# Addresses, one number of a build-time list and the pace of the modulation steps, in a two-layer decoder trunk on one core

## The chip, the cores and the metric

One NeuronCore of a Trainium2 chip runs the whole program. Its engines work side by side: TensorE (PE in the profile, with its weight loads as PEld), VectorE (DVE), ScalarE (ACT), GpSimd (POOL), and SyncE (SP), which issues the transfers from HBM. The metric is device microseconds of one execution.

## The reference

Two layers, 256 tokens, 1024 channels, everything in float32. In short:

```python
for l in range(DEPTH):                                   # DEPTH = 2
    mod = c_act @ w_ada[l] + b_ada[l]                    # 1024 x 6144, one row
    sh1, sc1, g1, sh2, sc2, g2 = split(mod, 6)
    h = rms_norm(x, norm1_g[l]) * (1 + sc1) + sh1
    q, k, v, iq, ik, iw, z, xbc, dt_raw, ga, gm = split(h @ w_in[l])      # 10856 columns
    o_attn = dsa_attention(...) @ w_attn_o[l]            # 64 keys kept of each query's causal ones
    o_ssm  = rms_norm((ssd_scan(...) + xs * d_skip) * silu(z)) @ w_ssm_o[l]
    x = x + g1 * ((sigmoid(ga) * o_attn + sigmoid(gm) * o_ssm) @ w_out[l])
    h = rms_norm(x, norm2_g[l]) * (1 + sc2) + sh2
    val, gate = split(causal_dwconv(h @ w_up[l]))        # 2 x 2816 columns
    x = x + g2 * ((silu(gate) * val) @ w_down[l])
```

## The kernel before, in words

**Products.** Every large weight matrix streams through once. A unit is a piece of 512 rows by 512 columns (four blocks of 128 rows); SP loads it into `st`. ScalarE rounds it to float32r (`wh`, line 783) and VectorE takes the rest (`wl = st - wh`, line 784). Both rings have three buffers:

```python
hi = wpool.tile([P, u["nk"], u["n"]], F32R, tag="wh", name=f"wh{cnt[0]}", bufs=3)
lo = wpool.tile([P, u["nk"], u["n"]], F32R, tag="wl", name=f"wl{cnt[0]}", bufs=3)
```

Activations are split in the same way, and each product of two float32 values is three matmuls: high by high, low by high, high by low. In `run_fm` the weights are the stationary operand and 256 tokens move (twelve matmuls for one block of 128 output columns in one unit); in `run_tm` the activations are stationary and 512 weight columns move. The program has 8112 such matmuls; below they are called products. Their order is fixed by the plan of the layers, so the number of products issued is a clock of the program that both versions share.

**The order of everything else** is made at build time. Each operation on ScalarE, VectorE and GpSimd becomes a `Work` with an estimated duration (`takes`), and `plan_ahead` lays these out in time on each engine against TensorE's own time `now`, which `on_pe` advances by a price for each matmul (`after`, line 392). For a float32r product of 256 columns this price was 9.5 + 0.4258 x 256 = 118.5 ns. `commit` then issues the work in the order of its planned starts. No duration of this list reaches the chip: it only decides the order in which instructions stand in each engine's queue, and each engine works through its own queue strictly in order.

**Side tasks** (turns of q and k by transposes, attention, the state-space part, norms) are generators. `pump`, called after every twelve products or so, resumes one when the list believes its operands ready (`Need.due`).

**Modulation.** Four of the twelve 512-column pieces of layer 0's `w_ada` are done at the start; the other 20 pieces (8 of layer 0, 12 of layer 1) run as a stream in the background, `ada_stream` at line 1011. A piece is eight steps: a 256 KB load `ad` and one VectorE operation `adacc = ad * c + adacc`. Then TensorE sums over the partitions (the fold, `bk<-adacc,ones`), ScalarE copies the row out (`adarow<-bk`), and TensorE turns it (`bk<-ident,adarow`). How many steps should be done by which pump is the table `GOALS` (line 714).

**Places in SBUF.** Tiles get fixed byte addresses by the order and the size of their allocation. In the built program, `wh` and `wl` start at 32 modulo 256 in every partition; the activations `h` (first norm's output and others) and `u` at 224, which is 192 further on; `xdt` (it also holds the last two operands of two products in each layer), `cbm` and `text` at 160; `ones` at 128.

Of the kernel before, what the change touches and what calls it, by code (L numbers as in the profile page):

```python
# [10 lines left out]
F32 = mybir.dt.float32  # L11
# [11 lines left out]
KT = 8  # L23
# [23 lines left out]
def trunk(ctx, tc, x, c, positions, w_ada, b_ada, norm1_g, w_in, q_norm_g, k_norm_g, ssm_conv_w, ssm_conv_b,  # L47
# [22 lines left out]
    class Work:  # L70


        __slots__ = ("key", "ns", "pr", "deps", "least", "start", "end", "done", "issue", "share", "soft")

        def __init__(self, key, ns, deps, least, issue):
            number[0] += 1
            self.key, self.ns, self.pr, self.deps, self.least = key, ns, number[0] - boost[0], deps, least
            self.start, self.end, self.done, self.issue = None, None, False, issue
            self.share, self.soft = 1.0, 0.0

    def region(x):

# [101 lines left out]
    def commit(edge=None):  # L184

        plan_ahead()
        edge = now[0] - LEAD_IN if edge is None else edge
        for key, ws in waiting.items():
            for w in sorted(ws, key=lambda w: w.start):
                if w.start < edge:  # L190
                    w.done = True
                    w.deps = ()
                    free_at[key] = max(w.start + 0.4 * w.ns, w.end - LAP[key])
                    if w.share < 1.0:
                        at_port[key == "pool"] = w
                    begun.append(w)
            ws[:] = [w for w in ws if not w.done]
        begun.sort(key=lambda w: (w.start, w.pr))
        n = 0
        while n < len(begun) and begun[n].start < edge:  # L200
            begun[n].issue()  # L201
            begun[n].issue = None
            n += 1
        del begun[:n]

    def end_of(w, by=None):
        if not w.done:
# [184 lines left out]
    def after(prev, cur):  # L392

        kind, n, shape = prev
        ns = 92.0 if shape != cur[2] else 0.0
        if kind == "r":
            return ns + 9.5 + 0.4258 * max(n, S)
        if kind in "bt":
            return ns + (2.5 + 0.832 * n if kind == "t" else 173.0)
        if shape == (128, 128):  # L400
            return ns + (143.0 if n <= 32 else 16.0 + 1.617 * n)
        if shape == (128, 32):
            return ns + 21.0
        return ns + (0.85 * n if shape == (128, 64) else 0.95 * n if n == S else 163.0)

    slow_until = [0.0]

    def on_pe(o, lhsT, rhs, issue, turn=False):
        n, rows, cols = rhs.free_size(), lhsT.partition_size(), lhsT.free_size()
# [80 lines left out]


    ident = cst.tile([P, P], F32, name="ident")
    ones = cst.tile([P, P], F32, name="ones")
    V.memset(ones, 1.0)
    G.affine_select(ident, ones, pattern=[[-1, P]], compare_op=ALU.is_equal, fill=0.0, base=0, channel_multiplier=1)
    mhalf = cst.tile([P, 2], F32, name="mhalf")
    G.memset(mhalf, -0.5)


# [33 lines left out]
    SP.dma_start(crow, c.rearrange("b (r q) -> (b r) q", q=P))  # L533
    pc = bank()
    T.transpose(pc[:, 0:KT], crow, ident[0:KT, 0:KT])
    csil = cst.tile([P, KT], F32, name="csil")
    gate_act = A.activation(csil, pc[:, 0:KT], AF.Tanh, scale=0.5)
    V.scalar_tensor_tensor(csil, csil, 1.0, pc[:, 0:KT], op0=ALU.add, op1=ALU.mult)
    chalf = cst.tile([P, KT], F32, name="chalf")
    V.tensor_scalar(chalf, csil, 0.5, None, op0=ALU.mult)  # L540
    crep = hold(w_tile("cv", [P, S])).rearrange("p (k n) -> p k n", n=32)
    crep_ins = V.tensor_scalar(crep, csil[:, :, None].to_broadcast([P, KT, 32]), 0.5, None, op0=ALU.mult)
# [4 lines left out]
    class Link:  # L547
# [73 lines left out]
        def finish(self, ev):  # L621

            def features(m, ps):
                settle(lambda: self.r is not None)
                bias = w_tile("bcol", [P, 1])
                if self.i == 0:
                    y = ev(m, None)
                    with urgent(FIRST):
                        V.tensor_scalar(bias, ps[:, S:S + 1], 0.5, None, op0=ALU.mult)
                        V.tensor_tensor(y, ps[:, 0:S], self.r, op=ALU.mult)  # L630
                        A.activation(y, y, AF.Tanh, scale=0.5, bias=bias)
                else:
# [78 lines left out]
    MARGIN = 11000.0  # L711


    GOALS = ((44, 0), (224, 50), (364, 98), (618, 147), (720, 161))
    LEAD = 6
    ADA_LATE = -30
    ADA_GAP = 7000.0
# [610 lines left out]
    def mixer(l, link, link_out):  # L1328
# [40 lines left out]
        def use_misc(ps):  # L1369
# [24 lines left out]
            def dt_task():  # L1394
# [29 lines left out]
                mm(pa[:, 0:32], uext[:, 0:P], adt[:, 0, 0:32], True, False)  # L1424
                mm(pa[:, 32:64], ones, adt[:, 0, 0:32], False, False)
                mm(pa[:, 32:64], uext[:, 0:P], adt[:, 1, 0:32], False, True)
                acs = w_tile("acs", [P, 2, 32], F32, 1)
                A.activation(acs.rearrange("p t h -> p (t h)"), pa[:, 0:64], AF.Copy)
                pb = bank()
                mm(pb[0:64, 0:S], adt[:, 0, :], uext, True, False)  # L1430
# [498 lines left out]
```

## Time and profile before

| | us |
|---|---|
| median of three runs (1241.02 to 1243.19) | 1241.21 |
| the profiled execution | 1240.05 |
| its span, from the first to the last instruction | 1238.3 |

| engine | busy us | share of the span | instructions |
|---|---|---|---|
| PE | 1206.7 | 97% | 9833 |
| PEld | 1122.9 | 91% | 9833 |
| DVE | 991.0 | 80% | 1549 |
| ACT | 776.7 | 63% | 1397 |
| POOL | 475.5 | 38% | 503 |

The profile lists rows of one engine as start, duration, engine, line, operation, what is written and what is read (`out<-in`), how many equal ones follow each other, and in brackets the engine's idle time before, with what ended it. Nearly all rows stand at L201, the line at which `commit` issues, so they are told apart by tile names. Matmuls overlap: what one costs is the distance from its start to the next start, not its duration. In layer 0 the first mixer runs from about 20 to 445 us and the FFN to 645 us; layer 1 follows, with its FFN from about 1045 us.

### The profile page before, as it was taken

The numbers are of one execution on the slowest core, as the hardware profiler recorded it, in microseconds if no ns is written. First come the engines' busy times: TensorE is split into PE (matmuls) and PEld (weight loads), VectorE is DVE, ScalarE is ACT, GpSimd is POOL, SyncE is SP. The second block draws the span as 40 slices with busy tenths as digits, with TensorE's granted clock in tenths as the row PEclk, the third lists the DMA queues.
The fourth block names the chain that finished last, engine by engine and source line by source line (L and its number), as shares of the span: only waits on it lengthen the run. The fifth ranks groups of instructions, "written<-read, shape, count | busy, mean of one in ns | idle before, by whom it ended". The sixth has DMA issues, their size and how long they took to land.

```text
span 1238.3 us, 24795 instructions
## 1 busy us (share of the span) xinstructions
PE 1206.7 (97%) x9833; PEld 1122.9 (91%) x9833; DVE 991.0 (80%) x1549; ACT 776.7 (63%) x1397; POOL 475.5 (38%) x503
## 2 busy tenths in 40 slices
PE   8999999999999999999999999999999999999898
PEld 7777888999999999999997777899999999999898
DVE  5599998877977789989777998888788677887762
ACT  4465667775774478776364566877588435877732
POOL 2162623342343226675121554405416222556510
PEclk9999999999999999999999999999999999999999
DMA  9854644556565748777847555444665665556551
GB/s 301 277 201 145 220 161 146 177 194 210 191 221 198 257 143 260 246 230 244 284 145 258 176 191 193 150 163 164 207 214 168 217 226 179 166 185 211 198 188 58
DMA packets 158665, 246.55 MB, mean 199 GB/s; under 512 B 11868, under 2 KB 66870, under 8 KB 158549
## 3 DMA queue, kind: packets, MB, share of 16 engines
q1 hardware_dynamic: 157989, 244.77, 59.6%
q8 instruction: 77, 1.26, 0.4%
q14 instruction: 39, 0.32, 0.1%
q0 software_dynamic: 288, 0.19, 0.1%
q10 hardware_dynamic: 272, 0.00, 0.0%
HBM read 243.89 MB, written 1.05 MB: 198 GB/s over the span
## 4 chain that ended last, share of the span: by engine, by line
PE 77%; DVE 12%; ACT 5%; POOL 3%; issue 3%; DMA 0%; DVEq 0%; ACTq 0%; POOLq 0%
PE bk L201 77%; DVE wl L201 5%; DVE w L201 3%; POOL w L201 2%; ACT wh L201 2%; ACT w L201 2%; DVE adacc L201 1%; DVE t L201 1%; DVE u L201 1%; POOL rr L201 0%; DVE mx L201 0%; ACT u L201 0%; DVE p L201 0%; POOL rows L201 0%; DVE sp_p L201 0%
## 5 line engine op out<-in xcount | busy, mean ns | idle before, releaser
L201 PE MATMUL bk<-h,wh 128*128 128x256 f32 x3296 | 591.5, 282 | 1.2 <-ACT h L201 1.1
L201 PEld LDWEIGHTS bk<-h,wh 128*128 128x128 f32 x3296 | 502.1, 189 | 11.4 <-issue 8.6
L201 DVE TENSOR_TENSOR wl<-st,wh 128x2048 fp32r<-128x2048 f32 (+1 forms) x200 | 440.5, 2209 | 84.5 <-ACT wh L201 84.1
L201 PE MATMUL bk<-h,wl 128*128 128x256 f32 x1648 | 459.5, 279 | 1.2 <-DVE wl L201 1.2
L201 ACT ACTIVATE wh<-st 128x2048 fp32r<-128x2048 f32 (+1 forms) x200 | 352.9, 1770 | 151.3 <-PE bk L201 117.6
L201 POOL TENSOR_TENSOR w<-w,w 128x254 f32<-128x254 f32 (+2 forms) x213 | 253.8, 1205 | 322.4 <-DVE w L201 223.7
L201 PEld LDWEIGHTS bk<-h,wl 128*128 128x128 f32 x1648 | 310.8, 189 | 2.8 <-DVE wl L201 2.4
L201 PE MATMUL bk<-u,wh 128*128 128x256 f32 x1312 | 233.4, 281 | 0.0
L201 PEld LDWEIGHTS bk<-u,wh 128*128 128x128 f32 x1312 | 199.4, 189 | 2.2 <-issue 2.2
L201 PE MATMUL bk<-u,wl 128*128 128x256 f32 x656 | 182.9, 279 | 0.0
L201 ACT ACTIVATE w<-bk,vec 128x256 f32<-128x256 f32 (+2 forms) x256 | 118.4, 519 | 55.7 <-DVE w L201 37.0
L201 PE MATMUL bk<-wh,h 128*128 128x512 f32 x448 | 146.6, 404 | 3.1 <-ACT wh L201 2.0
L201 PEld LDWEIGHTS bk<-u,wl 128*128 128x128 f32 x656 | 123.6, 188 | 0.0
L201 DVE SCALAR_TENSOR_TENSOR adacc<-ad,chalf,adacc 128x512 f32<-128x512 f32 x140 | 120.3, 860 | 2.7 <-DMA ad<-in_w_ada_dram 1.2
L201 PEld LDWEIGHTS bk<-wh,h 128*128 128x128 f32 x448 | 82.5, 189 | 24.1 <-issue 3.5
L201 DVE SCALAR_TENSOR_TENSOR w<-bk,vec,w 128x255 f32<-128x255 f32 (+1 forms) x176 | 79.9, 475 | 21.5 <-ACT w L201 19.6
L201 PE MATMUL bk<-wl,h 128*128 128x512 f32 x224 | 89.0, 397 | 3.0 <-DVE wl L201 3.0
L201 POOL TENSOR_TENSOR u<-u,u 128x256 f32<-128x256 f32 (+1 forms) x56 | 61.7, 1120 | 58.3 <-DVE u L201 30.4
L201 POOL TENSOR_TENSOR rr<-ss,mhalf 128x16 f32<-128x16 f32 x8 | 33.6, 4195 | 75.8 <-DVE ss L201 75.7
L201 ACT ACTIVATE u<-bk 128x128 f32<-128x128 f32 (+2 forms) x128 | 32.4, 327 | 36.3 <-PE bk L201 36.3
L201 PEld LDWEIGHTS bk<-wl,h 128*128 128x128 f32 x224 | 42.5, 190 | 13.3 <-DVE wl L201 4.5
L201 POOL TENSOR_SCALAR p<-p,sums 128x128 f32<-128x128 f32 x64 | 36.6, 590 | 33.9 <-DVE sums L201 33.9
(225 smaller groups left out, 1386.5 us busy)
## 6 DMA issues: line engine op xcount, KB each, us to landing
st<-in_w_in_dram SPq DMA_DIRECT2D x80, 1024.0 KB, 5.2
st<-in_w_up_dram SPq DMA_DIRECT2D x88, 512.0 KB, 4.7
ad<-in_w_ada_dram SPq DMA_DIRECT2D x160, 256.0 KB, 5.3
st<-in_w_down_dram SPq DMA_DIRECT2D x20, 1024.0 KB, 6.5
st<-in_w_ssm_o_dram SPq DMA_DIRECT2D x16, 1024.0 KB, 5.3
st<-in_w_ada_dram SPq DMA_DIRECT2D x16, 512.0 KB, 9.3
st<-in_w_attn_o_dram SPq DMA_DIRECT2D x8, 1024.0 KB, 5.1
st<-in_w_out_dram SPq DMA_DIRECT2D x8, 1024.0 KB, 5.2
```

The costliest lines, as they stand in the source:

```text
L201: begun[n].issue()
```

## The change

The diff has four parts.

- **Addresses.** Three small constants are allocated earlier, `bcol` gets eight buffers, `acs` is 80 instead of 64 wide, and a spacer of 256 bytes stands ahead of the `u` tiles. In the built program this moves `xdt`, `cbm` and `text` from 160 to 224 and `ones` from 128 to 224 modulo 256; `wh`, `wl`, `h` and `u` keep theirs.
- **The list's price of a product** falls from 118.5 to 114.0 ns (5.0 instead of 9.5).
- **`GOALS`**: 66 instead of 50 modulation steps by pump 224, and 98 by pump 350 instead of 364.
- **`commit`** issues an operation only after those it needs; before, equal or later planned starts of a needed one could stand behind.

```diff
-        begun.sort(key=lambda w: (w.start, w.pr))
-        n = 0
-        while n < len(begun) and begun[n].start < edge:
-            begun[n].issue()
...
+        for w in begun:
+            w.turn = w.start, w.pr
+        begun.sort(key=lambda w: w.turn)
+        while begun and begun[0].turn[0] < edge:
+            w = begun.pop(0)
+            late = [(d.turn or (d.start, d.pr))[0] for d in w.needs if d.issue]
+            if late:
+                w.turn = max(max(late), w.turn[0]) + 0.5, w.pr
+                insort(begun, w, key=lambda w: w.turn)
+                continue
+            w.issue()
...
-            return ns + 9.5 + 0.4258 * max(n, S)
+            return ns + 5.0 + 0.4258 * max(n, S)
...
+    mhalf = cst.tile([P, 2], F32, name="mhalf")
+    csil = cst.tile([P, KT], F32, name="csil")
+    chalf = cst.tile([P, KT], F32, name="chalf")
     ones = cst.tile([P, P], F32, name="ones")
...
-                bias = w_tile("bcol", [P, 1])
+                bias = w_tile("bcol", [P, 1], bufs=8)
...
-    GOALS = ((44, 0), (224, 50), (364, 98), (618, 147), (720, 161))
+    GOALS = ((44, 0), (224, 66), (350, 98), (618, 147), (720, 161))
...
+        pools["u"].tile([P, 64], F32, tag="front", name="front_u", bufs=1)
...
-                acs = w_tile("acs", [P, 2, 32], F32, 1)
+                acs = w_tile("acs", [P, 80], F32, 1)[:, 0:64].rearrange("p (t h) -> p t h", t=2)
```

All work stays the same; where it stands changes on every engine. Three places are shown. In the kernel before issued instructions stand at L201, in the changed one at L209; the numbers in the names differ between the versions.

The first is ScalarE's queue at the border of the layers, at the first full unit behind the 128-column pieces of layer 1 (the row with 128x2048). `wh` rows are splits, `u<-bk` rows copy q's turned index heads out of PSUM. Before:

```order
L201 ACTIVATE wh_8450<-st_8173 128x512
L201 ACTIVATE u_8481<-bk_8502 128x128
L201 ACTIVATE u_8482<-bk_8502 128x128
L201 ACTIVATE u_8483<-bk_8502 128x128
L201 ACTIVATE u_8484<-bk_8502 128x128
L201 ACTIVATE wh_8491<-st_8286 128x2048
```

Now, with the same split as `wh_8522`:

```order
L209 ACTIVATE wh_8476<-st_8192 128x512
L209 ACTIVATE wh_8522<-st_8306 128x2048
L209 ACTIVATE u_8512<-bk_8533 128x128
L209 ACTIVATE u_8513<-bk_8533 128x128
L209 ACTIVATE u_8514<-bk_8533 128x128
L209 ACTIVATE u_8515<-bk_8533 128x128
```

The split went ahead of the four copies. TensorE's queue at the same border, where `ident,t` rows are the transposes of a turned part of q. Before:

```order
L201 MATMUL bk_8489<-h_8285,wh_8450 128x256
L201 MATMUL bk_8489<-h_8284,wl_8451 128x256
L201 MATMUL bk_8522<-ident,t_1193_8487 128x128 x4
L201 MATMUL bk_8524<-wh_8491,h_8250 128x512
L201 MATMUL bk_8524<-wh_8491,h_8251 128x512
L201 MATMUL bk_8524<-wl_8492,h_8250 128x512
```

Now:

```order
L209 MATMUL bk_8520<-h_8305,wh_8476 128x256
L209 MATMUL bk_8520<-h_8304,wl_8477 128x256
L209 MATMUL bk_8552<-wh_8522,h_8269 128x512
L209 MATMUL bk_8552<-wh_8522,h_8270 128x512
L209 MATMUL bk_8552<-wl_8523,h_8269 128x512
L209 MATMUL bk_8552<-wh_8522,h_8272 128x512
L209 MATMUL bk_8552<-wh_8522,h_8273 128x512
L209 MATMUL bk_8552<-wl_8523,h_8272 128x512
L209 MATMUL bk_8592<-ident,t_1197_8518 128x128 x4
```

Four transposes that stood ahead of the full unit's first products stand behind six of them.

The second is ScalarE's queue at the last modulation row, in layer 1's FFN: `w<-bk` rows are the two taps of the FFN's convolution for four blocks of a chunk (`bk_14623` and `bk_14624` before hold two blocks each). Before:

```order
L201 ACTIVATE u_14604<-w_2105_14603 128x256
L201 ACTIVATE w_2114_14716<-bk_14623,vec_1593 128x256
L201 ACTIVATE w_2115_14717<-bk_14623,vec_1593 128x254
L201 ACTIVATE w_2116_14718<-bk_14623,vec_1593 128x256
L201 ACTIVATE w_2117_14719<-bk_14623,vec_1593 128x254
L201 ACTIVATE w_2118_14748<-bk_14624,vec_1593 128x256
L201 ACTIVATE w_2119_14749<-bk_14624,vec_1593 128x254
L201 ACTIVATE w_2123_14753<-bk_14624,vec_1593 128x256
L201 ACTIVATE w_2124_14754<-bk_14624,vec_1593 128x254
L201 ACTIVATE adarow_14775<-bk_14774 128x128
```

Now:

```order
L209 ACTIVATE w_2105_14604<-w_2103_14602 128x256
L209 ACTIVATE w_2114_14713<-bk_14621,vec_1560 128x256
L209 ACTIVATE w_2115_14714<-bk_14621,vec_1560 128x254
L209 ACTIVATE w_2116_14715<-bk_14621,vec_1560 128x256
L209 ACTIVATE w_2117_14716<-bk_14621,vec_1560 128x254
L209 ACTIVATE w_2118_14746<-bk_14622,vec_1560 128x256
L209 ACTIVATE w_2119_14747<-bk_14622,vec_1560 128x254
L209 ACTIVATE adarow_14770<-bk_14769 128x128
L209 ACTIVATE u_14605<-w_2105_14604 128x256
```

The row's copy stands behind six taps instead of eight, and the split of the activation `u` that stood ahead of them stands behind it.

The third is VectorE's queue in the first mixer, near product 1700 of 8112 (around 340 us before): the split of a unit's low part, `wl`, and what is ahead of it. Before, the unit of this place was split here:

```order
L201 SCALAR_TENSOR_TENSOR w_639_4093<-bk_3926,vec_293,w_639_4093 128x254
L201 SCALAR_TENSOR_TENSOR adacc_3974<-ad_3994,chalf,adacc_3974 128x512
L201 SCALAR_TENSOR_TENSOR u_4092<-w_637_4091,w_635_4089 128x256
L201 TENSOR_TENSOR wl_4117<-st_3840,wh_4116 128x2048
L201 TENSOR_TENSOR wl_4225<-st_3927,wh_4224 128x2048
```

Now:

```order
L209 SCALAR_TENSOR_TENSOR adacc_3854<-ad_4001,chalf,adacc_3854 128x512
L209 TENSOR_TENSOR p_650_4197<-p_650_4197,cbm_348_2159 128x768
L209 SCALAR_TENSOR_TENSOR u_4060<-w_628_4059,w_626_4057 128x256
L209 SCALAR_TENSOR_TENSOR w_640_4109<-bk_3925,vec_293,w_640_4109 128x255
L209 SCALAR_TENSOR_TENSOR w_640_4109<-bk_3925,vec_293,w_640_4109 128x254
L209 SCALAR_TENSOR_TENSOR adacc_3854<-ad_4052,chalf,adacc_3854 128x512
L209 SCALAR_TENSOR_TENSOR u_3673<-u_3673,dsk,bk_4284 128x256
L209 SCALAR_TENSOR_TENSOR u_4108<-w_638_4107,w_636_4105 128x256
L209 SCALAR_TENSOR_TENSOR u_4112<-w_642_4111,w_640_4109 128x256
L209 TENSOR_TENSOR wl_4134<-st_3831,wh_4133 128x2048
L209 SCALAR_TENSOR_TENSOR u_3725<-u_3725,dsk,bk_4314 128x256
L209 TENSOR_TENSOR wl_4223<-st_3926,wh_4222 128x2048
```

In the order of all engines' instructions `wl_4117` stood 55 products ahead of the first that reads it; `wl_4134` stands 4 ahead of its first reader.

## Rows read from the trace of the kernel before

**Rows 1.** The page's chain of work that ended last, by engine, line and tile, as shares of the span.

```profile
PE bk L201 77%; DVE wl L201 5%; DVE w L201 3%; POOL w L201 2%; ACT wh L201 2%; ACT w L201 2%; DVE adacc L201 1%; DVE t L201 1%; DVE u L201 1%; POOL rr L201 0%; DVE mx L201 0%; ACT u L201 0%; DVE p L201 0%; POOL rows L201 0%; DVE sp_p L201 0%
```

**Rows 2.** Who TensorE waited for, the first row of the view: us in total, times, longest.

```profile
PE bk L201 <- DVE wl L201: 4.1, 8, 1.6
```

**Rows 3.** Busy time by stretch of the span: us of the stretch, then PE, PEld, DVE, ACT and POOL busy (with instructions), the granted TensorE clock, DMA share, GB/s. The first stretch lies in the first mixer, the second in the first FFN.

```profile
320.00:380.00 60.00, 60.00 (x525) 56.19 (x524) 49.42 (x58) 40.83 (x74) 31.34 (x23) 1.00 0.60 208
445.00:510.00 65.00, 65.00 (x568) 64.34 (x567) 61.59 (x86) 51.54 (x87) 33.82 (x29) 1.00 0.65 207
```

**Rows 4.** Two groups of the page: line, engine, operation, shapes and count, then busy us and mean ns of one, and idle time before.

```profile
L201 DVE TENSOR_TENSOR wl<-st,wh 128x2048 fp32r<-128x2048 f32 (+1 forms) x200 | 440.5, 2209 | 84.5 <-ACT wh L201 84.1
L201 DVE SCALAR_TENSOR_TENSOR adacc<-ad,chalf,adacc 128x512 f32<-128x512 f32 x140 | 120.3, 860 | 2.7 <-DMA ad<-in_w_ada_dram 1.2
```

**Rows 5.** The fold at 533 us in the first FFN: VectorE's last two steps before it, TensorE's row, then the stretch before and the stretch behind, with columns as in rows 3.

```profile
531.16 1.99 DVE L201 SCALAR_TENSOR_TENSOR adacc<-ad,chalf,adacc 128x512 f32<-128x512 f32 x2
...
533.30 0.59 PE L201 MATMUL bk<-adacc,ones 128*32 128x128 f32 x8 [2.21 <-DVE adacc L201]
...
526.80:530.20 3.40, 3.40 (x32) 3.40 (x32) 3.15 (x5) 2.19 (x3) 3.29 (x4) 1.00 0.77 222
...
533.45:536.85 3.40, 3.40 (x22) 3.04 (x16) 3.40 (x5) 2.44 (x7) 2.92 (x2) 0.50 0.91 286
```

**Rows 6.** The border of the layers: ScalarE's rows, VectorE's rows and TensorE's rows around the first full unit, each in order of time, then two stretches with columns as in rows 3.

```profile
661.01 0.79 ACT L201 ACTIVATE u<-bk 128x128 f32<-128x128 f32 x4 [6.87 <-PE bk L201]
661.66 1.94 ACT L201 ACTIVATE wh<-st 128x2048 fp32r<-128x2048 f32 x1
...
659.79 0.68 DVE L201 TENSOR_TENSOR t<-bk,sint 128x512 f32<-128x512 f32 x1
663.63 2.29 DVE L201 TENSOR_TENSOR wl<-st,wh 128x2048 fp32r<-128x2048 f32 x1 [3.16 <-ACT wh L201]
...
658.98 0.40 PE L201 MATMUL bk<-h,wh 128*128 128x256 f32 x2
...
662.20 0.60 PE L201 MATMUL bk<-ident,t 128*128 128x128 f32 x4
663.65 0.73 PE L201 MATMUL bk<-wh,h 128*128 128x512 f32 x2 [0.85 <-ACT wh L201]
665.97 0.51 PE L201 MATMUL bk<-wl,h 128*128 128x512 f32 x1 [1.60 <-DVE wl L201]
...
666.55:669.95 3.40, 3.40 (x10) 2.62 (x9) 3.37 (x7) 1.91 (x1) 0.04 (x1) 0.50 0.84 279
670.00:673.40 3.40, 3.40 (x17) 2.77 (x16) 3.40 (x8) 0.14 (x1) 3.21 (x4) 1.00 0.95 304
```

**Rows 7.** Layer 1's mixer: the copies of the turned q on ScalarE, TensorE's wait for `adt` (the state-space decay), and its first attention scores of q's second half (`u,u`), which read those copies.

```profile
773.25 0.77 ACT L201 ACTIVATE u<-bk 128x128 f32<-128x128 f32 x4
...
765.69 0.83 PE L201 MATMUL bk<-uext,adt 128*64 128x256 f32 x4 [0.95 <-DVE adt L201]
...
773.57 0.70 PE L201 MATMUL bk<-u,u 64*128 64x256 f32 x4 [1.87 <-ACT u L201]
```

**Rows 8.** ScalarE ahead of the last modulation row, and TensorE's row that reads it, in order of time.

```profile
1158.03 2.55 ACT L201 ACTIVATE w<-bk,vec 128x256 f32<-128x256 f32 x6
1161.99 0.93 ACT L201 ACTIVATE w<-bk,vec 128x256 f32<-128x256 f32 x2 [1.41 <-DVE w L201]
1162.81 0.28 ACT L201 ACTIVATE adarow<-bk 128x128 f32<-128x128 f32 x1
...
1163.14 0.33 PE L201 MATMUL bk<-ident,adarow 128*128 128x128 f32 x1 [3.15 <-ACT adarow L201]
```

**Rows 9.** TensorE in order of time, at two places; the distance between starts is what counts, and a pair (x2) with the single row behind it makes three products. First layer 1's last product: six products of `u` and `t`, the 24 of `xdt`, 132 of `u` and `t`, and what follows. Then the first mixer, where 24 products of `h` stand between two rows of `text,sel`. The last two rows are groups of the page, the `xdt` products with `wh` and the `text,sel` matmuls, columns as in rows 4.

```profile
1198.00 0.39 PE L201 MATMUL bk<-u,wh 128*128 128x256 f32 x2
...
1198.68 0.40 PE L201 MATMUL bk<-xdt,wh 128*128 128x256 f32 x2
...
1201.53 0.40 PE L201 MATMUL bk<-u,wh 128*128 128x256 f32 x2
...
1217.09 0.60 PE L201 MATMUL bk<-ident,xt 128*128 128x128 f32 x4
...
1217.88 0.39 PE L201 MATMUL bk<-u,wh 128*128 128x256 f32 x2
...
1218.22 0.39 PE L201 MATMUL bk<-u,wh 128*128 128x256 f32 x2
...
221.13 0.40 PE L201 MATMUL bk<-text,sel 128*128 128x256 f32 x2
221.36 0.40 PE L201 MATMUL bk<-h,wh 128*128 128x256 f32 x2
...
224.19 0.40 PE L201 MATMUL bk<-text,sel 128*128 128x256 f32 x2
224.43 0.39 PE L201 MATMUL bk<-h,wh 128*128 128x256 f32 x2
...
227.15 0.40 PE L201 MATMUL bk<-text,sel 128*128 128x256 f32 x2
...
L201 PE MATMUL bk<-xdt,wh 128*128 128x256 f32 x128 | 24.3, 284 | 1.3 <-ACT xdt L201 1.2
...
L201 PE MATMUL bk<-text,sel 128*128 128x256 f32 x64 | 13.3, 289 | 0.0
```

More of the change, by code (lines that the diff above doesn't have):

```diff
@@ L70, in trunk @@
     class Work:
-        __slots__ = ("key", "ns", "pr", "deps", "least", "start", "end", "done", "issue", "share", "soft")
+        __slots__ = ("key", "ns", "pr", "deps", "least", "start", "end", "done", "issue", "share", "soft", "needs", "turn")
         def __init__(self, key, ns, deps, least, issue):
@@ L79, in __init__ @@
             self.share, self.soft = 1.0, 0.0
+            self.needs, self.turn = deps, None
     def region(x):
@@ L197, in commit @@
             ws[:] = [w for w in ws if not w.done]
-        begun.sort(key=lambda w: (w.start, w.pr))
-        n = 0
-        while n < len(begun) and begun[n].start < edge:
-            begun[n].issue()
-            begun[n].issue = None
-            n += 1
-        del begun[:n]
+        for w in begun:
[9 more added lines that the diff above has]
+            w.issue()
+            w.issue, w.needs = None, ()
     def end_of(w, by=None):
@@ L404, in after @@
         return ns + (0.85 * n if shape == (128, 64) else 0.95 * n if n == S else 163.0)
-    slow_until = [0.0]
+    slow_until, last_on_pe = [0.0], []
     def on_pe(o, lhsT, rhs, issue, turn=False):
@@ L424, in on_pe @@
         w = Work("pe", 0.0, (), 0.0, issue)
+        w.needs = deps + last_on_pe
+        last_on_pe[:] = [w]
         form[:] = [cur, at]
@@ L495, in trunk @@
     G.affine_select(ident, ones, pattern=[[-1, P]], compare_op=ALU.is_equal, fill=0.0, base=0, channel_multiplier=1)
-    mhalf = cst.tile([P, 2], F32, name="mhalf")
     G.memset(mhalf, -0.5)
@@ L535, in trunk @@
     T.transpose(pc[:, 0:KT], crow, ident[0:KT, 0:KT])
-    csil = cst.tile([P, KT], F32, name="csil")
     gate_act = A.activation(csil, pc[:, 0:KT], AF.Tanh, scale=0.5)
     V.scalar_tensor_tensor(csil, csil, 1.0, pc[:, 0:KT], op0=ALU.add, op1=ALU.mult)
-    chalf = cst.tile([P, KT], F32, name="chalf")
     V.tensor_scalar(chalf, csil, 0.5, None, op0=ALU.mult)
```

## The prediction

> **What bounds the kernel now.** I read the engine table first: TensorE is busy 1206.7 of 1238.3 us, 97%, VectorE 80%, ScalarE 63%. The reader is to see that only two things can pay here: the 31.6 us in which TensorE is not busy, and the distance between its products. The chain of waits says the same: 77% of it are TensorE's own rows, 5% VectorE's splits `wl` [rows 1]. The list of who TensorE waited for names `wl` first, 8 waits of 4.1 us together, the longest 1.6 [rows 2]. Then I read the stretches: VectorE has 10.6 of 60 us free in the first mixer, but 3.4 of 65 in the FFN [rows 3]. Last came the rows in order of time around each long wait, to see which instruction ended it and what stood ahead of that one in its queue.
>
> The profiled execution took 1240.05 us, 1.16 less than the median of 1241.21. The sum is made against 1240.05, and 1.16 is added at the end.
>
> **The change part by part.** The arithmetic keeps its instructions, so no engine is relieved as a whole. The `commit` rule, the price and `GOALS` cost nothing by themselves: they choose an order. What they bring is in the waits that come and go.
>
> *The border of the layers.* TensorE waited 0.85 us for `wh` and 1.60 for `wl` of the first full unit; `wh` began at 661.66, behind four copies that began at 661.01 [rows 6]. Now the split stands ahead of these copies. Then it needs only its ring buffer, which the products ahead of 658.98 read last: 658.98 + 1.94 = 660.9. VectorE's last `t` ends at 659.79 + 0.68 = 660.5, so `wl` runs from 660.9 to 660.9 + 2.29 = 663.2. TensorE, its four transposes moved behind, comes to the unit at 662.20 and wants `wl` two products later; before, these took 665.97 - 1.60 - 663.65 = 0.72, so at 662.9. It waits about 0.3 instead of 2.45. Behind the old wait lay a stretch of 3.4 us at a granted clock of 0.50, the lower of the two levels, with 10 matmuls where the next one has 17 [rows 6]: 7 x 0.2 = 1.4 us. TensorE had waited twice just before it fell. I count that as gone: 0.3 - 2.45 - 1.4 = -3.5. Bounds: 0, if the load or ScalarE's queue holds the split where it was, and -3.9.
>
> *The fold at 533 us.* TensorE waited 2.21 us for two `adacc` steps, and a stretch at 0.50 followed with 22 matmuls where an undisturbed one has 32 [rows 5]: 10 x 0.113 = 1.1. Together 3.3. `GOALS` takes two pieces, 16 steps of 0.86 us [rows 4] = 13.8 us, out of the FFN, where VectorE has 3.4 of 65 us free [rows 3], and in the new order four folds stand there, not six. I credit 70%: -2.3, between 0 (the wait stands at another fold) and -3.3.
>
> *The same 13.8 us in the first mixer.* It has 10.6 of 60 us free [rows 3], so over some 200 us the steps fit (35 us free) but not at every place. At the third place shown `wl_4134` stands 4 products ahead of its reader instead of 55. A split takes 2.21 us [rows 4], four products 0.46, so the wait is up to 1.75 us; I take +1.8, for what is late here has no cover. Behind that split is another `wl`, which is then late as well. Bounds: 0, if VectorE is ahead of the list on the chip, and 1.75 + 1.4 for a stretch at the lower level as at the border = 3.2.
>
> *Scores at 771.70.* TensorE waited 1.87 us for copies that ScalarE began at 773.25 [rows 7]. The scores now stand 36 products behind the turn they need, not 12: 24 x 0.115 (between the two steps of a product shown below) = 2.8 us, more than the wait. -1.7, between 0 and -1.9.
>
> *The last modulation row.* TensorE was ready at 1163.14 - 3.15 = 1159.99; the copy stood behind two taps that had waited 1.41 for VectorE [rows 8]. Behind six taps alone it ends at 1158.03 + 2.55 + 0.28 = 1160.86, a wait of 0.9, which gains 2.3. If the taps also start earlier, because the split of `u` no longer stands ahead, the whole 3.15 goes. -2.5.
>
> *`adt`.* Its wait of 0.95 [rows 7] goes, since the first matmul that reads it has 12 and 16 products of margin and had 4 and 5: 8 x 0.115 = 0.9. -0.9, bounds 0 and -0.95.
>
> *Addresses.* Products have two steps. From 1198.00 to 1198.68 six take 113.3 ns each; the 24 of `xdt` up to 1201.53 take 118.75; then 132 products of `u` and `t`, the same form as those before, take 15.56 us, 117.9 each, until four transposes end it: 1217.88 to 1218.22 is again 113.3 [rows 9]. So `xdt` at 128 from `wh` is slower itself and leaves the slow step to others. Moved to 192, as `u` is, it should inherit the step of what ran before it. There are 128 such products and half as many with `wl`, 192 in eight groups of 24: 192 x 5.4 = 1.0 us, of which I count 0.6, since part runs in slow surroundings where only 0.9 ns is to be had. The slow stretch behind is worth 132 x 4.6 = 0.6 at this place; for all eight groups I take 1.0, as most are followed by another interruption soon. `text,sel` is no such case: the pair at 221.13 is followed by 24 products of 117.9, the pair at 224.19, by the same operands, by 24 of 113.3 [rows 9]. What an interruption leaves depends on more than addresses. 32 pairs with 24 slow products behind each would be 32 x 24 x 4.6 = 3.5 us; I take a quarter, 0.9, and 0.5 for `ones`. Together -3.0. Bounds: +4, if new addresses leave the slow step where now a fast one is, and -11 (first rival).
>
> [...]
>
> *What I don't see.* So many rows move that new waits will come. An average `wl` wait is 4.1/8 = 0.5 us [rows 2]; four of them are +2.0. Bounds 0 and the third rival.
>
> Sum: -3.5 - 2.3 + 1.8 - 1.7 - 2.5 - 0.9 - 3.0 + 2.0 = -10.1. 1240.05 - 10.1 + 1.16 = 1231.1 us.
>
> **Rivals.** *The addresses do much.* For: one interruption sets over a hundred products [rows 9], and I estimate from the two places shown that half of the 8112 run at the slow step. 8112/2 x 4.6 ns = 18.7 us would be all; if the moved operands start 60% of it, -11 instead of -3: 1223.1. Against: `ident`, `adarow` and `p` interrupt as well and keep their places.
>
> *The waits only move.* In so long a list each long wait is an accident of order, and a new order has its own. For: nothing in the change aims at `adt`, `adarow` or the scores; they gain by chance. If all of the 10.9 us from the five waits comes back elsewhere and the addresses give 1 to 3, the time is 1238 to 1241; I take 1239.5.
>
> *Slower: modulation steps push splits late in the first mixer.* Place: between pump 44 and 224, where 66 steps stand instead of 50. Price: 1.75 us for each late `wl`, and 1.4 more where the clock falls to its lower level behind it: 3.2. With the addresses at 0 the gains are 10.9; from four such splits on (12.8) the kernel is slower, five give 16 - 10.9 = +5.1: 1246.3. For: VectorE's third place stands so already. Against: 10.6 of 60 us are free there, and `wl` has three buffers ahead.
>
> **Chances.** Forecast (1226 to 1237) 0.60, addresses do much 0.12, waits only move 0.18, late splits 0.10. 0.2%, 2.5 us, is about what a measurement of this kernel can tell from no change. Below 1238.7 lie the forecast, the first rival and 0.04 of the second: faster 0.76. Of the second 0.13 is no change that can be told, and 0.01 is slower, with the third rival 0.11. The range from 1220 to 1241 leaves out 0.05 of the first rival below and some 0.12 above.
>
> **What would show it.** In the profile of the changed kernel: no stretch at a granted clock of 0.50 near 533 and 666 us, and TensorE's wait at the first full unit under 1 us; no wait for `adarow` over 1 us near 1160 and none for `u` near 771; a wait for `wl` of 1 to 2 us near 335 us; no idle time for `adacc` in the FFNs; the 24 `xdt` products at the distance of the `u` products before them. Wrong would be: `xdt` products at 118 ns between `u` products of 113 (the address step), several `wl` waits over 1 us before 300 us (third rival), or a waiting list as long as before with other names (second).

## The result and the profile after

The changed kernel took 1228.66 us (1227.39 to 1230.05, 4 runs) beside 1242.19 of the kernel before on the same chip: a ratio of 0.9891, 95% interval 0.9874 to 0.9907. Timed again later beside three experiments, it took 1225.98 us beside 1243.63, a ratio of 0.9858 (0.9841 to 0.9874). Two measurements of one pair differ by 0.3%, and the times of one kernel go along with its granted clock (23 executions of the kernel before ran from 1239.70 us at a mean of 0.998 to 1247.03 at 0.994), so below only kernels that were timed in one go are compared that closely. The prediction was 1231.1 us, a gain of 10.1; measured are 13.5 us and, the second time, 17.7.

The profiled execution has a span of 1225.7 us instead of 1238.3. Its engine line, from the page:

```profile
PE 1201.3 (98%) x9835; PEld 1118.9 (91%) x9835; DVE 991.4 (81%) x1549; ACT 775.3 (63%) x1397; POOL 494.1 (40%) x503
```

TensorE is not busy for 1225.7 - 1201.3 = 24.4 us, 31.6 before: 7.2 us of waits went. It is also busy for 5.4 us less, with the same products. So the gain has two parts, and waits alone explain little over half. Taken up one by one below, the busy part is 4.1 us from faster products and 0.9 from stretches at the lower clock, of which one is left of two: 7.2 + 4.1 + 0.9 = 12.2 of the 12.6 us between the two spans.

Who TensorE waits for now (us, times, longest), against [rows 2]:

```profile
PE bk L209 <- DVE wl L209: 5.0, 6, 1.7
PE bk L209 <- DVE t L209: 2.5, 2, 2.0
...
PE bk L209 <- POOL t L209: 1.4, 1, 1.4
...
PE bk L209 <- DVE adacc L209: 0.9, 1, 0.9
PE bk L209 <- DVE adt L209: 0.8, 1, 0.8
...
PE bk L209 <- ACT adarow L209: 0.3, 1, 0.3
```

The waits for `adarow` (3.15) and for `u` (1.87) are gone, `adacc` and `adt` are shorter, and `wl` has grown.

The border of the layers, to be laid against [rows 6]: ScalarE, VectorE, GpSimd, TensorE, and the stretch behind the wait with columns as in rows 3.

```profile
663.31 1.92 ACT L209 ACTIVATE wh<-st 128x2048 fp32r<-128x2048 f32 x1 [4.81 <-PE bk L209]
...
665.26 3.08 DVE L209 TENSOR_TENSOR wl<-st,wh 128x2048 fp32r<-128x2048 f32 x1 [0.43 <-ACT wh L209]
...
664.91 1.29 POOL L209 TENSOR_TENSOR t<-t,t 128x512 f32<-128x512 f32 x1 [1.45 <-DVE t L209]
...
666.59 0.62 PE L209 MATMUL bk<-wh,h 128*128 128x512 f32 x2
668.40 0.50 PE L209 MATMUL bk<-wl,h 128*128 128x512 f32 x1 [1.19 <-DVE wl L209]
...
668.50:671.90 3.40, 3.40 (x18) 2.81 (x19) 3.37 (x3) 2.30 (x6) 0.00 (x0) 1.00 0.49 149
```

The split `wh` starts as soon as TensorE frees its buffer, no longer behind the copies. One wait of 1.19 us is left of two, and the clock stays at its upper level. The split `wl` took 3.08 us instead of 2.29, and the traces show where such long splits stand: in the fourteen profiled executions every one of the 1106 full splits (128x2048) with no GpSimd instruction running at the same time took 2.27 to 2.30 us, and all 430 that took over 2.6 ran in part beside a GpSimd operation on two tiles, here `t<-t,t`. (Not every split beside one is longer, and no run moved such an operation alone.)

The late split in the first mixer, named in the prediction by its place: VectorE's last modulation step ahead of it and the split, TensorE, and the two stretches behind.

```profile
338.13 0.74 DVE L209 SCALAR_TENSOR_TENSOR adacc<-ad,chalf,adacc 128x512 f32<-128x512 f32 x1
...
340.56 2.81 DVE L209 TENSOR_TENSOR wl<-st,wh 128x2048 fp32r<-128x2048 f32 x1
...
341.19 0.50 PE L209 MATMUL bk<-h,wh 128*128 128x256 f32 x2
343.43 0.39 PE L209 MATMUL bk<-h,wl 128*128 128x256 f32 x1 [1.74 <-DVE wl L209]
...
349.97 0.60 PE L209 MATMUL bk<-ident,u 128*128 128x128 f32 x4
...
344.70:348.10 3.40, 3.40 (x18) 2.52 (x17) 2.87 (x5) 0.42 (x1) 3.32 (x4) 0.51 0.96 341
348.20:351.60 3.40, 3.40 (x32) 3.40 (x32) 2.05 (x5) 0.00 (x0) 1.00 (x1) 1.00 1.04 393
```

TensorE's high products start unhindered, so `wh` was there; the split starts at 340.56, 1.1 us before TensorE wants its result (343.43 - 1.74 = 341.69), and takes 2.81. It costs 1.74 us and a stretch at the lower level with 18 matmuls where the next has 32: 14 x 0.113 = 1.6 us more. In e10 below, which has the same order, the wait is as long, 1.70 us, but what follows is done sooner; its rows for the product behind the wait and the four transposes that stand at 349.97 above:

```profile
347.31 0.38 PE L209 MATMUL bk<-h,wl 128*128 128x256 f32 x1 [1.70 <-DVE wl L209]
...
352.33 0.60 PE L209 MATMUL bk<-ident,u 128*128 128x128 f32 x4
```

That is 343.43 to 349.97, 6.54 us, against 5.02, so the stretch costs 1.5 us, and with one order it came in one of these two executions and not in the other.

The largest fold wait of the FFN, and the last modulation row [rows 5, 8]:

```profile
554.51 0.43 PE L209 MATMUL bk<-adacc,ones 128*32 128x128 f32 x8 [0.86 <-DVE adacc L209]
...
1148.41 2.55 ACT L209 ACTIVATE w<-bk,vec 128x256 f32<-128x256 f32 x6
1150.82 0.30 ACT L209 ACTIVATE adarow<-bk 128x128 f32<-128x128 f32 x1
...
1151.40 0.27 PE L209 MATMUL bk<-ident,adarow 128*128 128x128 f32 x1
```

The row's copy goes out behind six taps, and TensorE, which reads it at 1151.40, does not wait at all.

Products, against [rows 9]: the 24 of `xdt` in layer 1's last product, then three `text,sel` pairs in layer 1's mixer, then a pair in layer 0's that stands behind slow products.

```profile
1186.89 0.39 PE L209 MATMUL bk<-xdt,wh 128*128 128x256 f32 x2
...
1189.61 0.39 PE L209 MATMUL bk<-u,wh 128*128 128x256 f32 x2
...
818.32 0.39 PE L209 MATMUL bk<-text,sel 128*128 128x256 f32 x2
818.55 0.39 PE L209 MATMUL bk<-h,wh 128*128 128x256 f32 x2
...
821.27 0.39 PE L209 MATMUL bk<-text,sel 128*128 128x256 f32 x2
821.50 0.39 PE L209 MATMUL bk<-h,wh 128*128 128x256 f32 x2
...
824.22 0.39 PE L209 MATMUL bk<-text,sel 128*128 128x256 f32 x2
...
262.15 0.40 PE L209 MATMUL bk<-u,wh 128*128 128x256 f32 x2
...
263.21 0.39 PE L209 MATMUL bk<-text,sel 128*128 128x256 f32 x2
263.44 0.39 PE L209 MATMUL bk<-u,wh 128*128 128x256 f32 x2
...
264.46 0.39 PE L209 MATMUL bk<-u,wh 128*128 128x256 f32 x2
```

The `xdt` products take 2.72/24 = 113.3 ns where they took 118.75, and all 24 products between two `text,sel` pairs take 113.3. At 262.15 nine products take 1.06 us, 117.8 each, and the nine from 263.44 on, behind the pair, 1.02, again 113.3. Of the 32 pairs of the changed kernel 31 are followed by the fast step, seven of them behind slow products; in the kernel before 26 of 32 are followed by the slow one. For all kernels below I took from the trace the distance between starts of each product of `h`, `u`, `t` or `xdt` that has another directly behind it, at the upper clock level (some 6,790 of 8112). Above 115.4 ns, the slow step, are 45.6% before and 33.3% now; their sum above 113.3 ns each falls from 14.6 to 10.5 us.

### The profile page after: what moved, and what is told of

The parts are those of the page before. It is cut to its first block, busy times and chain, and to the rows that moved or that the text cites. A ratio compares the mean times of both kernels' runs of the same rounds, so it can differ in the third digit from the quotient of the medians.

```text
span 1225.7 us, 24837 instructions
## 1 busy us (share of the span) xinstructions
PE 1201.3 (98%) x9835; PEld 1118.9 (91%) x9835; DVE 991.4 (81%) x1549; ACT 775.3 (63%) x1397; POOL 494.1 (40%) x503
## 4 chain that ended last, share of the span: by engine, by line
PE 81%; DVE 12%; ACT 2%; issue 2%; POOL 1%; DMA 1%; SPq 0%; DVEq 0%; POOLq 0%; ACTq 0%
PE bk L209 81%; DVE wl L209 5%; DVE w L209 2%; DVE adacc L209 1%; ACT wh L209 1%; DVE p L209 1%; DVE u L209 1%; DVE t L209 1%; ACT w L209 1%; POOL rr L209 0%; DMA ad<-in_w_ada_dram 0%; POOL rows L209 0%; DVE top L209 0%; DVE mx L209 0%; POOL w L209 0%
## 5 line engine op out<-in xcount | busy, mean ns | idle before, releaser
L209 PE MATMUL bk<-h,wh 128*128 128x256 f32 x3296 | 588.1, 281 | 1.2 <-ACT h L209 1.1
L209 PEld LDWEIGHTS bk<-h,wh 128*128 128x128 f32 x3296 | 500.9, 189 | 12.0 <-issue 8.2
L209 DVE TENSOR_TENSOR wl<-st,wh 128x2048 fp32r<-128x2048 f32 (+1 forms) x200 | 439.8, 2206 | 67.3 <-ACT wh L209 67.0
L209 PE MATMUL bk<-h,wl 128*128 128x256 f32 x1648 | 457.9, 278 | 1.7 <-DVE wl L209 1.7
L209 ACT ACTIVATE wh<-st 128x2048 fp32r<-128x2048 f32 (+1 forms) x200 | 352.8, 1770 | 154.8 <-PE bk L209 129.9
L209 POOL TENSOR_TENSOR w<-w,w 128x254 f32<-128x254 f32 (+2 forms) x213 | 254.9, 1209 | 252.7 <-DVE w L209 173.4
L209 PEld LDWEIGHTS bk<-h,wl 128*128 128x128 f32 x1648 | 309.9, 188 | 2.4 <-DVE wl L209 1.9
L209 PE MATMUL bk<-u,wh 128*128 128x256 f32 x1312 | 232.6, 280 | 0.0
L209 PEld LDWEIGHTS bk<-u,wh 128*128 128x128 f32 x1312 | 199.3, 189 | 2.4 <-issue 2.4
L209 PE MATMUL bk<-u,wl 128*128 128x256 f32 x656 | 182.7, 278 | 0.6 <-DVE wl L209 0.6
L209 PE MATMUL bk<-wh,h 128*128 128x512 f32 x448 | 145.9, 402 | 3.1 <-DVE t L209 2.0
L209 ACT ACTIVATE w<-bk,vec 128x256 f32<-128x256 f32 (+2 forms) x256 | 119.7, 519 | 37.5 <-DVE w L209 26.0
L209 PEld LDWEIGHTS bk<-u,wl 128*128 128x128 f32 x656 | 123.2, 188 | 0.8 <-DVE wl L209 0.8
L209 DVE SCALAR_TENSOR_TENSOR adacc<-ad,chalf,adacc 128x512 f32<-128x512 f32 x140 | 119.0, 850 | 0.5
L209 PEld LDWEIGHTS bk<-wh,h 128*128 128x128 f32 x448 | 81.5, 188 | 23.9 <-issue 3.7
L209 POOL TENSOR_TENSOR u<-u,u 128x256 f32<-128x256 f32 (+1 forms) x56 | 74.1, 1348 | 63.1 <-DVE u L209 37.3
L209 PE MATMUL bk<-wl,h 128*128 128x512 f32 x224 | 88.7, 396 | 2.8 <-DVE wl L209 2.7
L209 DVE SCALAR_TENSOR_TENSOR w<-bk,vec,w 128x255 f32<-128x255 f32 (+1 forms) x176 | 80.3, 476 | 13.4 <-ACT w L209 11.9
L209 POOL TENSOR_TENSOR rr<-ss,mhalf 128x16 f32<-128x16 f32 x8 | 35.6, 4454 | 77.7 <-DVE ss L209 77.7
L209 POOL TENSOR_SCALAR p<-p,sums 128x128 f32<-128x128 f32 x64 | 35.6, 574 | 55.5 <-DVE sums L209 47.8
L209 ACT ACTIVATE u<-bk 128x128 f32<-128x128 f32 (+2 forms) x128 | 32.1, 321 | 39.8 <-PE bk L209 39.2
L209 PEld LDWEIGHTS bk<-wl,h 128*128 128x128 f32 x224 | 42.1, 188 | 13.4 <-DVE wl L209 4.6
```

The lines of the kernel that those rows point to most:

```text
L209: w.issue()
```

## The experiments

The table repeats the two figures for every kernel: us in which TensorE is not busy (span minus busy time of its page), and the slow share with the sum above 113.3 ns. They come from one profiled execution of each kernel, the ratio from all timed ones.

| kernel | ratio to before (95%) | not busy | slow steps | sum |
|---|---|---|---|---|
| before | 1 | 31.6 | 45.6% | 14.6 |
| changed; again | 0.9891; 0.9858 | 24.4; 24.7 | 33.3; 32.6% | 10.5; 10.3 |
| e1 new addresses, old order | 0.9969 (0.9954 to 0.9984) | 31.4 | 41.4% | 12.9 |
| e2 old addresses, new order | 0.9906 (0.9891 to 0.9921) | 24.7 | 49.5% | 15.9 |
| e3 old GOALS | 0.9985 (0.9969 to 1.0001) | 34.5 | 31.8% | 10.1 |
| e4 GOALS alone | 1.0012 (0.9998 to 1.0026) | 32.4 | 50.6% | 16.1 |
| e6 50 by 224, 98 by 350 | 0.9987 (0.9974 to 1.0000) | 33.9 | 34.1% | 10.7 |
| e7 66 by 224, 98 by 364 | 0.9966 (0.9952 to 0.9980) | 31.4 | 38.1% | 12.0 |
| e8 `u`, `xdt`, `cbm`, `text` at distance 128 | 0.9953 (0.9936 to 0.9969) | 23.4 | 57.2% | 21.4 |
| e9 62 steps | 0.9866 (0.9843 to 0.9888) | 23.2 | 40.4% | 12.7 |
| e10 `u` at distance 0 | 0.9934 (0.9915 to 0.9953) | 24.4 | 43.2% | 17.3 |
| e11 price 116 | 0.9896 (0.9873 to 0.9918) | 24.7 | 44.0% | 13.8 |
| e12 58 steps | 0.9868 (0.9848 to 0.9888) | 23.1 | 29.9% | 9.4 |

Timed together were e1 to e4; the second changed run with e6 to e8; e9 to e11; e12.

**Addresses or order (e1, e2).** e1 adds to the kernel before only the places; e2 gives the changed kernel the old ones. A spacer keeps `u` at 224 in both, and each engine's order is that of the kernel it starts from.

```diff
# e1, on the kernel before
     ident = cst.tile([P, P], F32, name="ident")
+    mhalf = cst.tile([P, 2], F32, name="mhalf")
+    csil = cst.tile([P, KT], F32, name="csil")
+    chalf = cst.tile([P, KT], F32, name="chalf")
     ones = cst.tile([P, P], F32, name="ones")
...
+        pools["u"].tile([P, 48], F32, tag="front", name="front_u", bufs=1)
-                acs = w_tile("acs", [P, 2, 32], F32, 1)
+                acs = w_tile("acs", [P, 80], F32, 1)[:, 0:64].rearrange("p (t h) -> p t h", t=2)
# e2, on the changed kernel: the reverse, with a spacer of [P, 80]
```

> The kernel before with the new addresses alone (xdt, cbm, text and ones at 224 modulo 256); every engine's order is that of before, row for row. Theory A (addresses and order each give a part; in the trace of the changed kernel 24 xdt products keep the step of the u products before them and every text,sel pair is followed by products of 113.3 ns): 4 to 6 us faster than before, about 1237, TensorE's waits as before (533, 662 to 666, 771 and 1160 us). Rival B (the order does it all, which step products take is chance): within 1.5 us of before. Rival C (the addresses do it all): 12 to 13 us faster, 1229.

> The changed kernel with the old addresses (xdt, cbm and text at 160, ones at 128), every engine's order as in the changed kernel. Theory A: 4 to 6 us slower than the changed kernel, about 1234, xdt products at 118.7 ns and products behind text,sel mostly at 117.9. Rival B: 1229. Rival C: 1241 to 1242.

e1 gained 0.31%, 3.9 us, just under the 4 to 6 expected, and kept its waits (31.4 us). e2 gained 0.94%, 11.7 us, and its products are slower than before (49.5%). Together 15.6 us, 1.25%, between the two measurements of the changed kernel. So both parts are real and add up within what was measured, theory A, with the order some three times the addresses. How much the addresses give is known roughly: e1's interval runs from 2.0 to 5.7 us, its profiled execution has the same span as that of before (1238.4 and 1238.3), and the sum of its slow steps fell by only 1.7 us; in the new order the same addresses take 15.9 - 10.5 = 5.4 us off that sum. In e1 the 24 `xdt` products of the last product:

```profile
1199.58 0.39 PE L201 MATMUL bk<-xdt,wh 128*128 128x256 f32 x2
...
1202.30 0.39 PE L201 MATMUL bk<-u,wh 128*128 128x256 f32 x2
```

2.72 us again, in the old order: it is the address that makes the step. (Of the other parts, the `commit` rule alone leaves the order of the kernel before as it was, row for row, and taken out of the changed kernel it changes nothing there either; the eight `bcol` buffers swap two rows of VectorE. So neither has a run of its own.)

**The distance itself (e8, e10).** Both take the changed kernel and move `u`, which most of `w_out` and `w_down` is multiplied by: e8 drops the wider `acs`, so that `u` (with `xdt`, `cbm` and `text`) lies 128 from the weights; e10 has a spacer of 80 instead of 64 columns, so that `u` lies at 32, distance 0, and the others stay.

> The changed kernel without the wider acs, so that u, xdt, cbm and text all lie at 160 modulo 256, 128 from wh and wl; the order is that of the changed kernel. If the distance of 128 makes a product slow (theory A): the 1968 products of u take 118 to 119 ns each instead of a mean of some 115, about 7 us, and with xdt and text 1237 to 1241. If what step products take is chance (rival B): 1228 to 1233, with u products at 113.3 in places.

> The changed kernel with the u tiles at 32 modulo 256, the place of wh and wl themselves (distance 0); xdt, cbm, text and ones stay at 224, the order is the same. If only a distance of 128 is bad: u products keep 113.3 and 117.9 as in the changed kernel, same time within 2 us. If 192 alone is good: u products at 118 to 120 ns and 8 to 12 us slower, as with u at 128.

In both, rows of `u` products late in layer 1's last product, e8 first:

```profile
1199.97 0.40 PE L209 MATMUL bk<-u,wh 128*128 128x256 f32 x2
...
1203.53 0.40 PE L209 MATMUL bk<-u,wh 128*128 128x256 f32 x2
```

```profile
1200.09 0.40 PE L209 MATMUL bk<-u,wh 128*128 128x256 f32 x2
...
1203.69 0.40 PE L209 MATMUL bk<-u,wh 128*128 128x256 f32 x2
```

Thirty products take 3.56 us at distance 128 (118.7 ns) and 3.60 at distance 0 (120.0 ns), while TensorE's waits are as in the changed kernel. e8 is 1238.02 beside 1225.98 us of the changed kernel timed with it. (Its profiled execution, 1233.81, was its fastest: 11.1 us more in slow steps, but no stretch at the lower clock behind the late split, at a mean clock of 0.999, where the changed kernel's had 0.998.) e10 lies 0.4 to 0.8% above the two ratios of the changed kernel, 5 to 9 us where 8 to 12 was expected. Chance (rival B) falls for good, and of the three distances tried only 192 gives 113.3 ns. The weights stood at 32 in all runs, so the distance and the place of the moving operand itself are not told apart.

**GOALS and price (e3, e4, e6, e7).** e3 and e4 take GOALS away from the changed kernel and give it alone to the one before; e6 and e7 undo one point of it each.

```diff
-    GOALS = ((44, 0), (224, 66), (350, 98), (618, 147), (720, 161))
+    GOALS = ((44, 0), (224, 50), (364, 98), (618, 147), (720, 161))   # e3
+    GOALS = ((44, 0), (224, 50), (350, 98), (618, 147), (720, 161))   # e6
+    GOALS = ((44, 0), (224, 66), (364, 98), (618, 147), (720, 161))   # e7
```

> The changed kernel with the old GOALS (50 steps by pump 224, 98 by 364). Theory A: GOALS takes away the wait of 2.2 us at 533 us with its slow-clock stretch and brings the one near 341 us with its own, so both about cancel: 1226 to 1231. If GOALS is what gains in the order: 1232 to 1236, with the wait for adacc back in the first FFN. If it costs (the late split at 341 us): 1223 to 1226.

> The kernel before with the new GOALS alone (old addresses, old price). Theory A: the fold's wait at 533 us goes (-3.3), a new wait for wl in the first mixer comes (+1.8 to +3), the waits at the border, for u at 771 and for adarow at 1160 stay, since they are the price's: 1239 to 1243. If GOALS is what gains: 1234 to 1238.

> The changed kernel with 50 modulation steps by pump 224 as before, but 98 by pump 350 as now. Theory D (the new price lets the pumps come to the end of layer 0 with too few steps done, so the piece that layer 1 needs is loaded when its fold is due; the extra 16 steps of the first mixer are what prevents it): in the order the last load of this piece still stands at the fold itself, so a wait for adacc of 2 to 5 us near 630 to 640 us, with a stretch at the lower clock: 1232 to 1238. Rival E (the point at 350 is what prevents it): no such wait, 1227 to 1231.

> The changed kernel with 66 steps by pump 224 as now, but 98 by pump 364 as before. Theory D: no late piece near 640 us, 1227 to 1232. Rival E: a wait for adacc of 5 us or more near 640 us, 1235 to 1242.

> The changed kernel as it is, beside the three that follow, so that they are compared on one chip: 1227 to 1231 for every theory.

I expected e3 within 1226 to 1231 us; it took 1241.67. Its longest wait was in no expectation. TensorE, SyncE's queue and the stretch from there:

```profile
639.83 0.66 PE L209 MATMUL bk<-adacc,ones 128*32 128x128 f32 x8 [10.57 <-DVE adacc L209]
...
627.38 6.31 SPq L209 DMA_DIRECT2D st<-in_w_in_dram  x3
633.79 5.00 SPq L209 DMA_DIRECT2D ad<-in_w_ada_dram  x5
...
632.30:645.90 13.60, 5.68 (x32) 5.26 (x33) 8.64 (x24) 3.77 (x10) 1.83 (x8) 0.50 0.40 116
```

The last five loads of the piece that layer 1's first norm needs are issued from 633.79 on, behind three weight loads that held SyncE's queue for 6.3 us, when TensorE already stands at the fold. It waits 10.57 us, and 13.6 us at the lower clock level begin within that wait. With 50 steps by pump 224 and the price of 114 the list leaves this piece undone until it is due; with the same table and the price of 118.5 the kernel before has no such wait. e6, with the point at 350 alone, has the same wait, shorter:

```profile
635.86 0.66 PE L209 MATMUL bk<-adacc,ones 128*32 128x128 f32 x8 [5.50 <-DVE adacc L209]
...
630.02 4.75 SPq L209 DMA_DIRECT2D st<-in_w_in_dram  x3
634.82 0.97 SPq L209 DMA_DIRECT2D ad<-in_w_ada_dram  x2
```

That is theory D's wait, somewhat longer than expected, and e6, with 1241.80 us, is 15.8 us slower than the changed kernel beside it and outside the 1232 to 1238 expected. The wait is a part of that only: TensorE is not busy for 9.2 us more, with waits of 1.27 and 1.59 us at the border, 1.80 for `adacc` at 578 us and 1.75 for `adarow` at 1155. e7 has no such wait, as theory D says, and yet it took 1239.52 us where 1227 to 1232 was expected. The first rows of its list:

```profile
PE bk L209 <- DVE wl L209: 8.0, 8, 3.0
PE bk L209 <- DVE t L209: 5.0, 3, 2.4
```

It lost to a wait of 3.0 us for `wl` behind the norm at the border, one of 2.4 for `t`, and four stretches at the lower level (two are 657.70 to 661.10 and 84.20 to 87.60 us, at 0.50), in a profiled execution (1242.58) that was the slowest of its twelve. So here neither theory held alone: the point at 224 keeps the piece in time, and moving the one at 350 brings other waits. GOALS alone (e4), with 1245.30 us where 1239 to 1243 was expected, gained nothing. Its `adarow` wait (3.23 us) stayed with the old price, as expected; the wait for `u` near 771 us and the border did not. First e4's split, the copies and TensorE's wait, then the same place of e3, which has the new price and the old table:

```profile
667.04 1.92 ACT L201 ACTIVATE wh<-st 128x2048 fp32r<-128x2048 f32 x1 [4.86 <-PE bk L201]
669.07 0.79 ACT L201 ACTIVATE u<-bk 128x128 f32<-128x128 f32 x4
...
672.07 0.51 PE L201 MATMUL bk<-wl,h 128*128 128x512 f32 x1 [1.21 <-DVE wl L201]
```

```profile
672.26 0.79 ACT L209 ACTIVATE u<-bk 128x128 f32<-128x128 f32 x4 [6.87 <-PE bk L209]
672.90 1.93 ACT L209 ACTIVATE wh<-st 128x2048 fp32r<-128x2048 f32 x1
```

In e4 the split went ahead of the copies with the old price, and in e3 it stayed behind them with the new one, with waits of 1.25 and 1.59 us. So the border's gain is not the price's, as e4's expectation has it; e11 below shows that it is not the table's alone either. What e4 won there it lost to a wait of 3.00 us for `wl` at 654 us, with 6.8 us at the lower clock, and to new `adacc` waits; the late split of the first mixer did not come.

**Is it one lucky order? (e9, e11, e12).** Three more orders near the changed one: 62 and 58 steps by pump 224, and a price of 116.0 (`ns + 7.0`).

> The changed kernel with 62 instead of 66 modulation steps by pump 224. In its order the split wl that the changed kernel issues 4 products ahead of its reader (near 341 us) no longer stands so late, and from layer 1 on the order is that of the changed kernel. Theory F (an order is worth what its few long waits and the low-clock stretches behind them cost): the 1.7 us at 341 us and the stretch at the lower clock behind it go, 2.5 to 3.5 us faster than the changed kernel, 1.5 to 1.7% faster than before. Rival G (something else ends last there, or a new wait comes for it): within 1 us of the changed kernel.

> The changed kernel with a price of 116.0 instead of 114.0 ns for a product in the list. Theory F: the late split at 341 us goes (-3), but the split wl of the first full unit of layer 1 stands 2 products ahead of its reader, a wait of 2 us near 665 us with a stretch at the lower clock (+3): 1226 to 1231. If the gain comes from a price near the true step, so that each ns back costs its share: half way back, 1234 to 1238.

> The changed kernel with 58 instead of 66 modulation steps by pump 224. In its order the last load of the piece that layer 1 needs is issued 85 products ahead of its fold, where with 50 steps it was issued at the fold. If that one late piece is what made 50 steps slow (theory D): no wait for adacc over 1.5 us near 630 us, 1223 to 1229, as with 62 and 66. If the gain of 66 and 62 steps is luck of two orders: anywhere up to 1240, with long waits at other places.

All three keep the gain: 1225.44, 1229.30 and 1225.65 us. In e9 the wait at 341 us and the low stretch are gone (no `wl` wait is over 1.2 us, and 344.0 to 347.4 us ran at a clock of 1.00), and TensorE is not busy for 23.2 instead of 24.4 us; but 40.4% of its products run at the slow step instead of 33%, which gives 2.2 us back, and the ratio lies between the two of the changed kernel. Theory F named the waits that went, but the time it forecast (1.5 to 1.7% under before, measured 1.34%) left out the steps. e11 has the expected wait for `wl` at the border (1.60 us, with 0.83 for `wh` and the low stretch) in place of the one at 341 us; 2 ns of the price back cost nothing like half of the gain. e12 has no wait for `adacc` over 1.5 us near 630 us, the longest anywhere is 0.5: the late piece goes between 50 and 58 steps. No version was found that beats the changed kernel clear of the 0.3%.

## Why the prediction was right, point by point

The time was forecast 2.4 us too high and the cause is the one given: waits that go by a new order, and a step of products that goes by addresses. That the sum came so near is in part luck: the terms below are off by 0.2 to 1.5 us in both directions, and short waits that no term had went as well. By its terms:

- *Border, -3.5.* Measured -2.7: the waits fell from 2.45 to 1.19, and the low stretch (1.4) went. The term was mis-sized by one number: I took 2.29 us for `wl`, and it took 3.08, beside a GpSimd operation that had been over before the split in the old order.
- *Fold at 533 us, -2.3.* The wait fell to 0.86 at another fold and the low stretch went: -1.35 - 1.1 = -2.5. But the reason given, that two pieces fewer relieve VectorE in the FFN, is not what the runs bear out: e4 does the same with the old price and has `adacc` waits of 3.9 us in all, the longest of 1.51 in the FFN, at 539 us; e3 keeps the old table and has no `adacc` wait at all ahead of the one at 640 us.
- *Late split near 340 us, +1.8.* The wait was 1.74, at the place named, but by two errors that cancel: the split had a lead of 1.13 us, not 0.46, and took 2.81 us, not 2.21, again beside a GpSimd operation (`u<-u,u`, from 339.43 to 341.23). The low stretch behind, in the bounds but not in the value, makes it 3.3.
- *Scores, modulation row, `adt`, together -5.1.* All of 1.87 and 3.15 went, and 0.95 of `adt`: -6.0. The taps did start earlier.
- *Addresses, -3.0.* e1 gives -3.9, and the products of the changed kernel 14.6 - 10.5 = 4.1. The parts were weighed wrongly: I said that the `text,sel` pairs are no such case and counted a quarter. With the new addresses pair after pair leaves 113.3 behind it, in e1 and, in 31 of 32 cases, in the changed kernel, whatever step it found. The `xdt` products do what was forecast: they keep the step that they find (113.3 ns behind 113.3 at 1186.89 us, 117.8 behind 117.8 at 602.31). In these rows `xdt`, like `u`, is the operand that moves and `wh` the stationary one. Of the eight groups of 24 `xdt` products four stand as four times six, with other products between.
- *What I don't see, +2.0.* New were 1.36 for `t` on GpSimd, 0.9 more for `t` at 80 us, 0.6 and 0.5 elsewhere, 3.4 together; short waits that no term had went as well (0.7 for `sums`, three of 0.33 for `wl` in the last FFN).

The step that failed outright is one sentence: that price and GOALS cost nothing by themselves and that each can be reckoned from the waits it removes. e3, e4, e6 and e7 show that they work only as a pair. The new price with the old table brings a wait of 10.57 us at the fold of layer 1's piece, the new table with the old price brings nothing, and the third rival's picture of the price of a late step was right in kind, but at another place: the dear one was not a `wl` split in the first mixer but a load at the end of the layer or, in e4 and e7, a split of 3.0 us behind the norm there.

## What to carry to other kernels

Where TensorE is 97% busy, look at the distance between its equal matmuls as well as at the waits: here two steps 4% apart were worth some 4 us by the places of a few operands, beside 12 us from the order, and a wrong place for `u` and three smaller ones cost 12. When a list made at build time changes its idea of TensorE's pace, try the tables that were tuned beside it again: here neither price nor table gained without the other. Check what is loaded last before each point where a result is needed, and in which queue it stands. A VectorE split with no slack is best not put beside a GpSimd operation on two tiles (all 430 splits over 2.6 us ran in part beside one, those beside none took at most 2.30); that is read from the traces, not tested. An order near a good one may remove a known wait and still not be faster, so time several.

## What was not expected of the hardware

- `u` at distance 0 modulo 256 from the weights was no better than at 128: 120.0 ns a product in e10 and 118.7 in e8, over thirty each; steps of 113.3 stand at 192. Other distances were not tried, and the weights were not moved.
- At distance 192 products ran at two steps, 113.3 and 117.9 ns, and stayed at one for long: in the changed kernel up to 563 in a row at the fast step (from 1073 us) and 273 at the slow one (from 558 us). Behind a `text,sel` pair stood the fast step in 31 of 32 cases with `text` at 224 (changed kernel), the slow one in 26 of 32 with `text` at 160 (before). What sets the step after a stall or a transpose stays open; the difference was worth 2.2 us between e9 and the changed kernel (12.7 and 10.5 us of slow steps).
- After one wait of one length the clock fell in one execution and not in another. TensorE waited 2.02 us for the same `t` near 80 us in the changed kernel and in e7; the first stretch below, of the changed kernel, is at the upper level, the second, of e7, at the lower. This wait (1.99 to 2.02 us) stands in eleven of the traces, and the clock fell behind it in three.

```profile
83.00:86.40 3.40, 3.40 (x21) 2.78 (x19) 2.21 (x4) 1.19 (x5) 2.99 (x1) 1.00 0.31 89
```

```profile
84.20:87.60 3.40, 3.40 (x12) 2.73 (x11) 2.23 (x4) 0.20 (x2) 2.93 (x1) 0.50 0.23 59
```
